# Gate columns of an mLSTM layer moved from a weight slab of their own into the first value slab

## The chip, the core and the metric

The kernel runs on one core of one Trainium2 chip. The metric is the device time of one execution in microseconds (us), as a median of runs. Three runs of the kernel before took 798.25, 798.49 and 798.56 us. Engines are named as the profile names them: PE multiplies matrices (PEld is its loading of the stationary operand), DVE is VectorE, ACT is ScalarE, POOL is GpSimd, and SP issues the weight loads.

## What is computed

Two transformer-like blocks run one after the other over 256 tokens of width 1024, in float32. The first has differential attention, retention, an MLP and a per-layer embedding. The second has an mLSTM, an up projection with a causal convolution, and a down projection. The change lies in the mLSTM's input projection. Cut to what matters, the reference is:

```python
proj = x @ w_in                      # [256, 1024] @ [1024, 3080]
q = proj[..., :512] * dqk ** -0.5    # 4 heads of 128
k = proj[..., 512:1024]
v = proj[..., 1024:2048]             # 4 heads of 256
o_gate = sigmoid(proj[..., 2048:3072])
log_i = proj[..., 3072:3076] + b_gates[:4]                # 8 gate columns
log_f = log_sigmoid(proj[..., 3076:] + b_gates[4:])
# from log_i and log_f: running sums and maxima over the tokens, which give
# the decay that weights the scores q k^T of each head before they meet v
```

The input `x` of this projection is normalized. The norm's factor, one number per token, is not put on `x` but on the products: queries, keys, values and gates are each multiplied by it when they are taken out of PSUM.

## The kernel before

**Weights.** All weights stream through the chip once, in slabs. A slab is 1024 rows by 256 columns and comes in two halves of 512 KB, each with 4 row blocks of 128 rows. `_plan` lists the slabs in the order of use, and `order` lists the halves. A half goes through three rings of buffers: `raw` (5 buffers, filled by SP's load, L151), `hi` (6 buffers: ACT writes the part that a float32r product keeps, L163) and `lo` (6 buffers: DVE writes the rest, L175). A load may start when the `lo` of the half five places earlier is done, and a `hi` or `lo` when PE has used the half six places earlier. Each product is done in three matmuls: high times high, low activations times high weights, and high activations times low weights.

**Order of the work.** Nothing is reordered at run time: each engine works through its instructions as they were written out. `step_b` keeps a block of weights stationary and streams 256 tokens (the result has features on partitions: queries, keys, gates); `step_a` keeps the activations stationary and streams 256 weight columns (the result has tokens on partitions: values). After each half `slot` writes out the next high and low parts and advances what the other engines have pending. `joint` runs two slabs whose last row blocks come late. It leaves its closing work, the statistic of the norm and the taking out of its two products, to a `tail` that is written out after the first half of the next slab.

**Around the change.** `joint(["mq0", "mk0"], ...)` makes the first queries and keys. The next slab, `mg`, holds the 8 gate columns alone, padded to 64 columns, in two loads of 128 KB. In its middle the tail multiplies the sums of squares with a matrix of ones (`pv_n4`, L981 and L982). From `pv_n4` DVE and ACT make the factor of the norm: `m4`, `v5`, a logarithm and an exponential on ACT, one Newton step, `rr` and `rrq` (L989 to L997). Only then can DVE take the first queries and keys out of PSUM (`post_scaled`, L538: `mqk<-ps_mq`, `mqk<-ps_mk`). After `mg` come `mq1`, `mk1` and four value slabs `mv0` to `mv3`. The gates go through `post_mg`, `gates2` (running sums), `gates3` (small transposes to tokens on partitions, `acol`) and, behind `mv1`, `decay_pe` and `decay_post` (the weights `dm` of the scores). The scores of heads 0 and 1 also come behind `mv1`, and meet the values (`my0`, `my1`) behind `mv3`.

**PSUM.** It has 8 banks; the kernel gives 4 to `mmbank` (the products of slabs) and 4 to `aux` (everything small). Within each kind the banks go round: the fifth request gets the bank of the first, and its first matmul has to wait until that bank has been read. Here `ps_mg` is an `aux` bank, so the products that follow the slab pairs take `mmbank`s in the order `pg2`, `pg3`, `mq0`, `mk0`, `mq1`, `mk1`, `mv0`, ...

Of the kernel before, what the change touches and what calls it, by code (L numbers as in the profile page):

```python
# [37 lines left out]
def _plan():  # L38
    slabs = []
    index = {}  # L40

    def slab(name, w, k0, nk, cl):
        index[name] = len(slabs)
        slabs.append((name, w, k0, nk, cl))

    for j in (0,):
        slab("q0", "w_in", 0, 8, 0)
        slab("k0", "w_in", 0, 8, 1024)
    for j in range(4):
# [12 lines left out]
    for j in range(16):  # L62
        slab(f"f1_{j}", "w_ff1", 0, 8, 256 * j)
    for j in range(4):
        for kg in range(4):
            slab(f"f2_{j}_{kg}", "w_ff2", 8 * kg, 8, 256 * j)
    slab("wp", "w_ple", 0, 2, 0)
    for j in range(4):
        slab(f"pg{j}", "w_ple_gate", 0, 8, 256 * j)
    for n in ("mq0", "mk0", "mg", "mq1", "mk1"):  # L70
        if n == "mg":
            slab("mg", "l0_mlstm_w_in_2", 0, 8, 3072)
        else:
            slab(n, "l0_mlstm_w_in_2", 0, 8, (512 if n[1] == "k" else 0) + 256 * int(n[2]))
# [24 lines left out]

@with_exitstack  # L100
def block_kernel(ctx: ExitStack, tc: tile.TileContext, I, out):
# [114 lines left out]
    def pe_b(ps, i, xh, xl, ks, m, start, stop):  # L216
        """A block of weights stays, the activations pass: out is [features, tokens]."""
# [12 lines left out]
    def pe_a(ps, i, xh, xl, ks, t, start, stop):  # L230
        """The activations stay, the weights pass: out is [tokens, features]."""
# [22 lines left out]
    def after(i, *posts):  # L254
        """The small products due behind slab i; what follows it on the other engines."""
# [8 lines left out]
    def halves(i, piece):  # L264
        for s in range(2):
# [77 lines left out]
    with tc.manual_schedule():  # L343
        S.preload_act_table_set(LNEXP)
# [640 lines left out]
        def r4_post():  # L985
            # with 1 / r4^2 = m4 + eps, both norms are (m5 + eps (m4 + eps))^-0.5
# [21 lines left out]
        def post_mg(ps):  # L1008
            gi = wk("gi", 384, tag="aT")[0:4, 0:T]
            gf = wk("gf", 384, tag="aT")[0:4, 0:T]  # L1010
            V.tensor_tensor(out=gi, in0=ps[0:4, 0:T], in1=rr[0:4, :], op=ALU.mult)
            V.tensor_tensor(out=gf, in0=ps[32:36, 0:T], in1=rr[32:36, :], op=ALU.mult)
            V.tensor_scalar(out=gi, in0=gi, scalar1=par[0:4, goff["gates"]:goff["gates"] + 1], scalar2=None, op0=ALU.add)
            V.tensor_scalar(out=gf, in0=gf, scalar1=par[0:4, goff["gates"] + 1:goff["gates"] + 2], scalar2=None, op0=ALU.add)
# [121 lines left out]
        def xnorm():  # L1136
            # x becomes the first block's output
# [22 lines left out]
        for j in range(4):  # L1160
# [54 lines left out]
        def h7_split(j):  # L1215
            """The normalized input; the first slabs take the input as it is and their products the factor."""
# [209 lines left out]
def _columns(a):  # L1426
    """A vector with its entries down the partitions: [128, n / 128]."""
# [3 lines left out]
def _packed(inputs):  # L1431
# [3 lines left out]
    gates[0:4] = f["l0_mlstm_b_gates_2"].reshape(2, 4).T  # L1435
# [5 lines left out]
    for h, (i, s) in enumerate(order):  # L1441
        name, key, k0, nk, cl = slabs[i]
        kk, cw = nk // 2, 2048 // nk
        m = f[key][0] if f[key].ndim == 3 else f[key]
        rows = m[(k0 + s * kk) * P:(k0 + (s + 1) * kk) * P]
        if name == "mg":
            v = w[h, :, 0:256].reshape(P, kk, 64)
            g = rows[:, cl:cl + 8].reshape(kk, P, 8).transpose(1, 0, 2)
            v[:, :, 0:4], v[:, :, 32:36] = g[:, :, 0:4], g[:, :, 4:8]
        else:  # L1450
            w[h] = rows[:, cl:cl + cw].reshape(kk, P, cw).transpose(1, 0, 2).reshape(P, kk * cw)
# [26 lines left out]
```

## Time and profile before

| what | value |
|---|---|
| runs | 798.25, 798.49, 798.56 us; median 798.49 |
| span of the profiled execution, first to last instruction | 796.7 us, mean granted clock 0.998 |
| runs' median less this span | 1.8 us |
| PE busy | 787.4 us, 99% |
| DVE busy | 570.3 us, 72% |
| ACT busy | 464.2 us, 58% |
| weights loaded | 140.25 MB on SP's queue |
| `mg` on PE | from 507.74 us, `mq1` follows at 511.42 us |

The profiled execution's own total is not given apart from its span; the 1.8 us between the span and the median of the runs lie around the instructions. A time such as 507.74 is counted from the first instruction of the span. In a row of the timeline the first number is the start, the second the duration, both in us; the duration of a matmul includes its way through the array, so what one costs is the distance to the start of the next. "x2" joins neighbours of the same kind, and what stands in brackets is idle time ahead of the row and what ended it.

### The profile page before, as it was taken

To read this page: it belongs to the slowest core of one execution; us is meant where nothing else is said; L and a number is where in the kernel's file an instruction comes from. 1 tells how busy PE (TensorE), PEld (TensorE's weight loads), DVE (VectorE), ACT (ScalarE), POOL (GpSimd) and SP (SyncE) were. 2 spreads that over 40 slices of the span, in tenths; PEclk is the share of its full clock that TensorE was granted. 3 is DMA by queue.
4 is the path that set the end of the run, shared out by engine and by line. 5 is a ranking of instruction groups with operands and counts; after the bars stand their busy time and mean duration, and the time that the engine had idled before them with its cause. 6 is when DMAs were issued, how large, how long until landed. Compare 5 with 4: busy or idle time off the path is not lost.

```text
span 796.7 us, 15746 instructions
## 1 busy us (share of the span) xinstructions
PE 787.4 (99%) x6416; PEld 773.2 (97%) x6416; DVE 570.3 (72%) x898; ACT 464.2 (58%) x785; POOL 1.9 (0%) x7
## 2 busy tenths in 40 slices
PE   8999999999999999999999999999999999999996
PEld 8999999999999999999999999999999999999885
DVE  6976889566666577666555557897978988987443
ACT  7655656765744456555444456755865766756432
POOL 0000000000000000000000000000000000000000
PEclk9999999999999999999999999999999999999999
DMA  8775454555666556665666645465374457765621
GB/s 297 274 238 164 151 158 129 149 161 162 188 196 187 172 181 195 190 188 188 199 185 188 181 145 166 136 205 169 121 220 160 143 178 235 221 203 166 206 80 53
DMA packets 40615, 141.97 MB, mean 178 GB/s; under 512 B 4656, under 2 KB 5296, under 8 KB 40544
## 3 DMA queue, kind: packets, MB, share of 16 engines
q1 hardware_dynamic: 40176, 140.25, 55.7%
q8 instruction: 50, 0.82, 0.4%
q0 software_dynamic: 224, 0.72, 0.2%
q14 instruction: 21, 0.17, 0.1%
q10 hardware_dynamic: 144, 0.00, 0.0%
HBM read 139.91 MB, written 1.05 MB: 177 GB/s over the span
## 4 chain that ended last, share of the span: by engine, by line
PE 97%; ACT 1%; DMA 1%; issue 0%; DVE 0%; SPq 0%
PE ps_f L227 8%; PE ps_f L226 8%; PE ps_f L228 8%; PE ps_uv L226 3%; PE ps_ug L226 3%; PE ps_ug L227 3%; PE ps_uv L227 3%; PE acc L1313 3%; PE acc L1315 3%; PE acc L1314 3%; PE ps_ug L228 3%; PE ps_uv L228 3%; PE ps_vr L238 1%; PE ps_va L238 1%; PE ps_mo L238 1%; PE ps_wo L227 1%
## 5 line engine op out<-in xcount | busy, mean ns | idle before, releaser
L175 DVE TENSOR_TENSOR lo_f<-raw_f,hi_f 128x1024 fp32r<-128x1024 f32 x64 | 77.7, 1222 | 52.9 <-ACT hi_f L163 52.9
L163 ACT ACTIVATE hi_f<-raw_f 128x1024 fp32r<-128x1024 f32 x64 | 67.6, 1060 | 79.6 <-PE ps_f L227 70.3
L227 PE MATMUL ps_f<-al,hi_f 128*128 128x256 f32 x256 | 72.1, 282 | 0.0
L226 PE MATMUL ps_f<-ah,hi_f 128*128 128x256 f32 x256 | 72.0, 281 | 0.0
L228 PE MATMUL ps_f<-ah,lo_f 128*128 128x256 f32 x256 | 72.0, 281 | 0.0
L226 PE MATMUL ps_f<-h2h,hi_f 128*128 128x256 f32 x256 | 71.9, 281 | 0.0
L227 PE MATMUL ps_f<-h2l,hi_f 128*128 128x256 f32 x256 | 71.9, 281 | 0.0
L228 PE MATMUL ps_f<-h2h,lo_f 128*128 128x256 f32 x256 | 71.8, 281 | 0.0
L226 PEld LDWEIGHTS ps_f<-ah,hi_f 128*128 128x128 f32 x256 | 48.3, 189 | 0.0
L228 PEld LDWEIGHTS ps_f<-ah,lo_f 128*128 128x128 f32 x256 | 48.3, 189 | 0.0
L226 PEld LDWEIGHTS ps_f<-h2h,hi_f 128*128 128x128 f32 x256 | 48.3, 189 | 0.0
L227 PEld LDWEIGHTS ps_f<-al,hi_f 128*128 128x128 f32 x256 | 48.2, 188 | 0.0
L227 PEld LDWEIGHTS ps_f<-h2l,hi_f 128*128 128x128 f32 x256 | 48.1, 188 | 0.0
L228 PEld LDWEIGHTS ps_f<-h2h,lo_f 128*128 128x128 f32 x256 | 48.1, 188 | 0.0
L175 DVE TENSOR_TENSOR lo_dn<-raw_dn,hi_dn 128x1024 fp32r<-128x1024 f32 x22 | 26.9, 1223 | 22.8 <-ACT hi_dn L163 22.8
L163 ACT ACTIVATE hi_dn<-raw_dn 128x1024 fp32r<-128x1024 f32 x22 | 23.3, 1061 | 30.7 <-PE acc L1314 24.5
L226 PE MATMUL ps_ug<-h7h,hi_ug 128*128 128x256 f32 x144 | 40.8, 283 | 0.0
L226 PE MATMUL ps_uv<-h7h,hi_uv 128*128 128x256 f32 x144 | 40.5, 282 | 0.0
L227 PE MATMUL ps_uv<-h7l,hi_uv 128*128 128x256 f32 x144 | 40.3, 280 | 0.0
L227 PE MATMUL ps_ug<-h7l,hi_ug 128*128 128x256 f32 x144 | 40.3, 280 | 0.0
L228 PE MATMUL ps_ug<-h7h,lo_ug 128*128 128x256 f32 x144 | 40.0, 278 | 0.0
L228 PE MATMUL ps_uv<-h7h,lo_uv 128*128 128x256 f32 x144 | 40.0, 278 | 0.0
(490 smaller groups left out, 2940.9 us busy)
## 6 DMA issues: line engine op xcount, KB each, us to landing
raw_f<-in_w_dram SPq DMA_DIRECT2D x64, 512.0 KB, 3.6
raw_ug<-in_w_dram SPq DMA_DIRECT2D x22, 512.0 KB, 4.2
raw_uv<-in_w_dram SPq DMA_DIRECT2D x22, 512.0 KB, 4.3
raw_dn<-in_w_dram SPq DMA_DIRECT2D x22, 512.0 KB, 3.8
raw_va<-in_w_dram SPq DMA_DIRECT2D x8, 512.0 KB, 5.2
raw_vr<-in_w_dram SPq DMA_DIRECT2D x8, 512.0 KB, 3.5
raw_gr<-in_w_dram SPq DMA_DIRECT2D x8, 512.0 KB, 3.5
raw_ga<-in_w_dram SPq DMA_DIRECT2D x8, 512.0 KB, 3.6
```

The source lines that it names most:

```text
L163: S.activation(hi_t[i, s], raw_t[i, s], ACTF.Copy)
L175: V.tensor_tensor(out=lo_t[i, s], in0=raw, in1=hi_t[i, s].bitcast(F32), op=ALU.subtract)
L226: TE.matmul(o, lhsT=hv[:, a, sl], rhs=xh[:, x, :], start=st, stop=False, skip_group_check=True)
L227: TE.matmul(o, lhsT=hv[:, a, sl], rhs=xl[:, x, :], start=False, stop=False, skip_group_check=True)
L228: TE.matmul(o, lhsT=lv[:, a, sl], rhs=xh[:, x, :], start=False, stop=sp, skip_group_check=True)
L238: TE.matmul(o, lhsT=xh[:, k, ts], rhs=hv[:, a, :], start=st, stop=False, skip_group_check=True)
L1313: TE.matmul(o, lhsT=gh[b][:, r, ts], rhs=hv[:, 0, ns], start=k == 0, stop=False)
L1314: TE.matmul(o, lhsT=gl[b][:, r, ts], rhs=hv[:, 0, ns], start=False, stop=False)
L1315: TE.matmul(o, lhsT=gh[b][:, r, ts], rhs=lv[:, 0, ns], start=False, stop=k == NK - 1)
```

## The change

The slab `mg` is gone. The 8 gate columns stand behind the 256 columns of the first value slab `mv0`, which is now 264 columns wide and comes third, straight behind `mq0` and `mk0`. A raw buffer holds 1024 columns, so this slab is loaded in three pieces, of 3, 3 and 2 row blocks (792, 792 and 528 columns), where the others have two. `step_wide` runs it as `step_a` does, with a bank of PSUM for each half of the tokens, both from `mmbank`. The gates now come out with tokens on partitions: four small ACT copies scale them into `gtok`, and two transposes on PE in the middle of `mk1` turn them. The rest of the gates' work moves back by one place, and the decay and the first scores stand behind `mv2` where they stood behind `mv1`; they still meet the values behind `mv3`.

```diff
-    for n in ("mq0", "mk0", "mg", "mq1", "mk1"):
-        if n == "mg":
-            slab("mg", "l0_mlstm_w_in_2", 0, 8, 3072)
...
-    for j in range(4):
-        slab(f"mv{j}", "l0_mlstm_w_in_2", 0, 8, 1024 + 256 * j)
+    for n in ("mq0", "mk0", "mv0", "mq1", "mk1", "mv1", "mv2", "mv3"):
+        slab(n, "l0_mlstm_w_in_2", 0, 8, {"q": 0, "k": 512, "v": 1024}[n[1]] + 256 * int(n[2]))
...
+def _rows(slab):
+    name, w, k0, nk, cl = slab
+    return ((0, 1, 2), (3, 4, 5), (6, 7)) if name == "mv0" else (tuple(range(nk // 2)), tuple(range(nk // 2, nk)))
+
+def _width(slab):
+    return 264 if slab[0] == "mv0" else 2048 // slab[3]
...
+    def step_wide(name, xh, xl):
+        i = index[name]
+        kk, cw = geometry(i)
+        pss = [mmbank(f"ps_{name}_{t}") for t in range(2)]
+        def piece(s):
+            for t in range(2):
+                ts = slice(t * P, (t + 1) * P)
+                for a, k in enumerate(_rows(slabs[i])[s]):
+                    hv, lv = hi_t[i, s], lo_t[i, s]
+                    o = pss[t][:, 0:cw]
+                    TE.matmul(o, lhsT=xh[:, k, ts], rhs=hv[:, a, :], start=k == 0, stop=False, skip_group_check=True)
+                    TE.matmul(o, lhsT=xl[:, k, ts], rhs=hv[:, a, :], start=False, stop=False, skip_group_check=True)
+                    TE.matmul(o, lhsT=xh[:, k, ts], rhs=lv[:, a, :], start=False, stop=k == 7, skip_group_check=True)
+        halves(i, piece)
+        after(i)
+        return pss
...
-        def post_mg(ps):
+        gtok = wk("gtok", 128, bufs=1)
+        nc.gpsimd.memset(gtok, 0.0)
+        gtokv = gtok.rearrange("p (t n) -> p t n", t=2)
+        def gates0(pss):
+            for t in range(2):
+                for q in range(2):
+                    S.activation(gtokv[:, t, 32 * q:32 * q + 4], pss[t][:, T + 4 * q:T + 4 * q + 4], ACTF.Copy, scale=rrc[:, t:t + 1])
+        def gates1_pe():
+            pg = aux("pg_t")
+            for t in range(2):
+                TE.transpose(pg[0:64, t * P:(t + 1) * P], gtokv[:, t, :], ident)
+            gt["pg"] = pg
...
-        at("mk1", col_pe("c5", rr))
-        at("mk1", col_post("c5", rrc))
-        at("mq1", None, gates2)
-        at("mv0", gates3_pe, gates3_post)
+        def mv0_tail(pss):
+            col_pe("c5", rr)()
+            i = index["mq1"]
+            later(i, col_post("c5", rrc))
+            later(i, lambda: gates0(pss))
+            later(i, lambda: post_halves(mvh, mvl, rrc, [pss[t][:, 0:T] for t in range(2)]))
...
+        at("mk1", gates1_pe, gates1_post, mid=True)
+        at("mk1", None, gates2)
+        at("mv1", gates3_pe, gates3_post)
...
-        for j, n in enumerate(("mv1", "mv1")):
+        for j, n in enumerate(("mv2", "mv2")):
...
-        mlstm(0, "mv1", "mv3")
+        mlstm(0, "mv2", "mv3")
...
-        mlstm(1, "mv1", "mv3")
+        mlstm(1, "mv2", "mv3")
...
-        step_b("mg", h4h, h4l, post_mg)
+        pss0 = step_wide("mv0", h4h, h4l)
+        tails.append((index["mq1"], lambda: mv0_tail(pss0)))
         step_b("mq1", h4h, h4l, post_scaled(mqt, 1, rrq))
```

The instructions of PE between the joint slabs and `mq1`, with the engines that each waits for in brackets; of equal neighbours only the first is shown. `hi_mg_0` is the high part of the gate slab's first half, `ps_mq1` the bank of the second queries. Before:

```order
L228 MATMUL ps_mk0_6160<-h4h_5832,lo_mk0_1_6074 128x256
L226 MATMUL ps_mg_6299<-h4h_5832,hi_mg_0_6102 64x256
L981 MATMUL pv_n4_6312<-sqs_n4_6197,ones_95 128x256 [waits DVE_49]
L982 MATMUL pv_n4_6312<-sqs_n5_6203,ones_95 128x256 [waits DVE_49]
L226 MATMUL ps_mg_6299<-h4h_5832,hi_mg_1_6185 64x256 [waits Activation_49]
L226 MATMUL ps_mq1_6355<-h4h_5832,hi_mq1_0_6233 128x256 [waits Activation_49]
```

Now:

```order
L232 MATMUL ps_mk0_6162<-h4h_5832,lo_mk0_1_6074 128x256
L317 MATMUL ps_mv0_0_6301<-hi_mv0_0_6102,h4h_5832 128x264 [waits PE_49]
L1004 MATMUL pv_n4_6321<-sqs_n4_6199,ones_95 128x256 [waits DVE_49]
L1005 MATMUL pv_n4_6321<-sqs_n5_6205,ones_95 128x256 [waits DVE_49]
L317 MATMUL ps_mv0_0_6301<-hi_mv0_1_6187,h4h_5832 128x264 [waits Activation_49]
L317 MATMUL ps_mv0_0_6301<-hi_mv0_2_6235,h4h_5832 128x264 [waits Activation_49]
L230 MATMUL ps_mq1_6382<-h4h_5832,hi_mq1_0_6253 128x256 [waits DVE_49,PE_49,Activation_49]
```

24 matmuls of `mg` made way for 48 of `mv0`, and the first matmul of `mq1`, which waited for ACT alone (its high part), now waits for DVE and PE as well: `mv0` took the two `mmbank`s that `mq1` and `mk1` had, so `mq1` gets the bank of `mq0`. In the built program this wait is for DVE's instruction `mqk<-ps_mq0`, which reads that bank.

DVE from the end of the statistic (`sqs_n5`) to that instruction; `m4` is the start of the factor's chain, whose eight instructions up to `rrq` are the same in both and are shown by `m4` and `rrq`. Before:

```order
L412 TENSOR_TENSOR sqs_n5_6203<-sqa_n5_5835 128x256
L175 TENSOR_TENSOR lo_mg_1_6205<-raw_mg_1_5972,hi_mg_1_6185 128x256
L175 TENSOR_TENSOR lo_mq1_0_6235<-raw_mq1_0_6007,hi_mq1_0_6233 128x1024
L175 TENSOR_TENSOR lo_mq1_1_6253<-raw_mq1_1_6039,hi_mq1_1_6251 128x1024
L175 TENSOR_TENSOR lo_mk1_0_6295<-raw_mk1_0_6076,hi_mk1_0_6293 128x1024
L989 COPY m4_6315<-pv_n4_6312 128x256
L997 TENSOR_SCALAR rrq_6130<-rr_6128 128x256
L538 TENSOR_TENSOR mqk_6134<-ps_mq0_6159,rrq_6130 128x512
```

Now:

```order
L435 TENSOR_TENSOR sqs_n5_6205<-sqa_n5_5835 128x256
L179 TENSOR_TENSOR lo_mv0_1_6207<-raw_mv0_1_5972,hi_mv0_1_6187 128x792
L179 TENSOR_TENSOR lo_mv0_2_6237<-raw_mv0_2_6007,hi_mv0_2_6235 128x528
L179 TENSOR_TENSOR lo_mq1_0_6255<-raw_mq1_0_6039,hi_mq1_0_6253 128x1024
L179 TENSOR_TENSOR lo_mq1_1_6297<-raw_mq1_1_6076,hi_mq1_1_6295 128x1024
L1012 COPY m4_6324<-pv_n4_6321 128x256
L1020 TENSOR_SCALAR rrq_6130<-rr_6128 128x256
L561 TENSOR_TENSOR mqk_6136<-ps_mq0_6161,rrq_6130 128x512
```

Ahead of `m4` stood a low part of 256 columns and three of 1024; now there stand one of 792, one of 528 and two of 1024.

DVE some 10 us earlier, between the squares of the first four feature blocks and the low parts of the next two (`h4l`). Before:

```order
L409 TENSOR_TENSOR sqa_n5_5835<-sqa_n5_5835,sq_n5_1_6119 128x512
L175 TENSOR_TENSOR lo_mg_0_6123<-raw_mg_0_5920,hi_mg_0_6102 128x256
L959 TENSOR_TENSOR pgs2_6072<-pgs2_6072,pw_5754 128x512
L961 TENSOR_TENSOR x0_73<-x0_73,pgs2_6072 128x512
L953 TENSOR_TENSOR pgs3_6145<-ps_pg3_6041,r3_5755 128x512
```

Now:

```order
L432 TENSOR_TENSOR sqa_n5_5835<-sqa_n5_5835,sq_n5_1_6119 128x512
L179 TENSOR_TENSOR lo_mv0_0_6123<-raw_mv0_0_5920,hi_mv0_0_6102 128x792
L982 TENSOR_TENSOR pgs2_6072<-pgs2_6072,pw_5754 128x512
L984 TENSOR_TENSOR x0_73<-x0_73,pgs2_6072 128x512
L976 TENSOR_TENSOR pgs3_6147<-ps_pg3_6041,r3_5755 128x512
```

The low part in second place has 792 columns where it had 256. On ACT the high part `hi_mv0_0` likewise has 792 columns where `hi_mg_0` had 256; it stands ahead of these squares.

More of the change, by code (lines that the diff above doesn't have):

```diff
@@ L93, in _plan @@
         if n not in paired:
-            order += [(i, 0), (i, 1)]
+            order += [(i, s) for s in range(len(_rows(slabs[i])))]
         elif any(n == g[0] for g in JOINT):
@@ L140, in geometry @@
     def geometry(i):
-        name, w, k0, nk, cl = slabs[i]
-        return nk // 2, 64 if name == "mg" else 2048 // nk
+        return len(_rows(slabs[i])[0]), _width(slabs[i])
     def dma_to(n):
@@ L146, in dma_to @@
             i, s = order[state["dma"]]
-            name, w, k0, nk, cl = slabs[i]
-            kk, cw = geometry(i)
+            name = slabs[i][0]
+            kk, cw = len(_rows(slabs[i])[s]), _width(slabs[i])
             raw = wpool.tile([P, 1024], F32, tag="raw", name=f"raw_{name}_{s}", bufs=NRAW)
@@ L158, in high_to @@
             i, s = order[state["high"]]
-            kk, cw = geometry(i)
+            kk, cw = len(_rows(slabs[i])[s]), _width(slabs[i])
             dma_to(state["high"] + 1)
@@ L169, in split_to @@
             i, s = order[state["split"]]
-            kk, cw = geometry(i)
+            kk, cw = len(_rows(slabs[i])[s]), _width(slabs[i])
             high_to(state["split"] + 1)
@@ L264, in halves @@
     def halves(i, piece):
-        for s in range(2):
+        for s in range(len(_rows(slabs[i]))):
             need(i, s)
@@ L280, in step_b @@
         i = index[name]
-        ps = (aux if name == "mg" else mmbank)(f"ps_{name}")
-        nm = 1 if name == "mg" else 2
+        ps = mmbank(f"ps_{name}")
         def piece(s):
-            for m in range(nm):
-                pe_b(ps, i, xh, xl, range(4 * s, 4 * s + 4), m, s == 0 and m == 0, s == 1 and m == nm - 1)
+            for m in range(2):
+                pe_b(ps, i, xh, xl, range(4 * s, 4 * s + 4), m, s == 0 and m == 0, s == 1 and m == 1)
         halves(i, piece)
@@ L1006, in block_kernel, with gates1_post @@
         gt = {}
-        def post_mg(ps):
+        gtok = wk("gtok", 128, bufs=1)
[10 more added lines that the diff above has]
+            gt["pg"] = pg
+        def gates1_post():
+            pg = gt.pop("pg")
             gi = wk("gi", 384, tag="aT")[0:4, 0:T]
             gf = wk("gf", 384, tag="aT")[0:4, 0:T]
[L1011 to L1014, printed above, removed]
+            V.tensor_scalar(out=gi, in0=pg[0:4, 0:T], scalar1=par[0:4, goff["gates"]:goff["gates"] + 1], scalar2=None, op0=ALU.add)
+            V.tensor_scalar(out=gf, in0=pg[32:36, 0:T], scalar1=par[32:36, goff["gates"] + 1:goff["gates"] + 2], scalar2=None, op0=ALU.add)
             l = wk("gl", 512, tag="qt")[0:4, 0:T]
@@ L1140, in xnorm, with post_halves @@
                                        op0=ALU.mult, op1=ALU.mult)
-        at("mk1", col_pe("c5", rr))
-        at("mk1", col_post("c5", rrc))
-        at("mq1", None, gates2)
-        at("mv0", gates3_pe, gates3_post)
+        def mv0_tail(pss):
[4 more added lines that the diff above has]
+            later(i, lambda: post_halves(mvh, mvl, rrc, [pss[t][:, 0:T] for t in range(2)]))
+        def post_halves(dh, dl, rc, pts):
+            for t in range(2):
+                S.activation(dh[:, t, 0:T], pts[t], ACTF.Copy, scale=rc[:, t:t + 1])
+            yield
+            for t in range(2):
+                V.scalar_tensor_tensor(out=dl[:, t, 0:T], in0=pts[t], scalar=rc[:, t:t + 1], in1=dh[:, t, 0:T].bitcast(F32),
+                                       op0=ALU.mult, op1=ALU.subtract)
+        at("mk1", gates1_pe, gates1_post, mid=True)
+        at("mk1", None, gates2)
+        at("mv1", gates3_pe, gates3_post)
         at("mo0", None, r4_late)
-        for j, n in enumerate(("mv1", "mv1")):
+        for j, n in enumerate(("mv2", "mv2")):
             at(n, lambda j=j: decay_pe(j), lambda j=j: decay_post(j))
-        mlstm(0, "mv1", "mv3")
+        mlstm(0, "mv2", "mv3")
         mlstm(2, "mv3", "mo0")
         mlstm(3, "mv3", "mo0")
-        mlstm(1, "mv1", "mv3")
+        mlstm(1, "mv2", "mv3")
         at("mo1", None, xnorm)
@@ L1156, in block_kernel @@
         joint(["mq0", "mk0"], h4h, h4l, r4_pe, r4_post, [post_scaled(mqt, 0, rrq), post_scaled(mkt, 0, rr)])
-        step_b("mg", h4h, h4l, post_mg)
+        pss0 = step_wide("mv0", h4h, h4l)
+        tails.append((index["mq1"], lambda: mv0_tail(pss0)))
         step_b("mq1", h4h, h4l, post_scaled(mqt, 1, rrq))
         step_b("mk1", h4h, h4l, post_scaled(mkt, 1, rr))
-        for j in range(4):
+        for j in range(1, 4):
             step_a(f"mv{j}", h4h, h4l, post_tok_split(mvh, mvl, j, rrc, 514 * (j // 2) + 258 * (j % 2)))
@@ L1434, in _packed @@
     gates = np.zeros((P, 2), np.float32)
-    gates[0:4] = f["l0_mlstm_b_gates_2"].reshape(2, 4).T
+    gates[0:4] = gates[32:36] = f["l0_mlstm_b_gates_2"].reshape(2, 4).T
     par = [_columns(f[n]) for n, _ in GAINS]
@@ L1442, in _packed @@
         name, key, k0, nk, cl = slabs[i]
-        kk, cw = nk // 2, 2048 // nk
+        ks, cw = _rows(slabs[i])[s], _width(slabs[i])
+        kk = len(ks)
         m = f[key][0] if f[key].ndim == 3 else f[key]
[L1445 to L1451, printed above, removed]
+        rows = m[(k0 + ks[0]) * P:(k0 + ks[0] + kk) * P]
+        cols = rows[:, cl:cl + cw] if name != "mv0" else np.concatenate([rows[:, cl:cl + T], rows[:, 3072:3080]], axis=1)
+        w[h, :, 0:kk * cw] = cols.reshape(kk, P, cw).transpose(1, 0, 2).reshape(P, kk * cw)
     return {
```

2 lines of the change are left out of this document (removed).

## The prediction

> **What bounds the kernel now.** I read first the page's busy shares and its chain, then PE's waits.
>
> ```profile
> PE 787.4 (99%) x6416; PEld 773.2 (97%) x6416; DVE 570.3 (72%) x898; ACT 464.2 (58%) x785; POOL 1.9 (0%) x7
> ...
> PE 97%; ACT 1%; DMA 1%; issue 0%; DVE 0%; SPq 0%
> ```
> ```profile
> PE ps_q L226 <- ACT hi L443: 1.2, 2, 0.8
> ```
>
> PE is busy for 787.4 of 796.7 us, the chain that ended last is 97% PE, and the longest wait between products is 0.8 us, at the start. So time is PE's instructions plus PE's pauses: a matmul less is a gain, and any wait put in front of PE is a loss in full. The span (796.7) and the median of the runs (798.49) differ by 1.8 us around the instructions; I make the sum on the span and add the same difference.
>
> **What PE saves and gains.** First the stretch of `mg`, on PE's timeline, then two rows that price a matmul of 258 columns and two that price a pair of transposes.
>
> ```profile
> 507.74 0.28 PE L226 MATMUL ps_mg<-h4h,hi_mg 128*64 128x256 f32 x1
> ...
> 509.15 0.59 PE L981 MATMUL pv_n<-sqs_n,ones 128*128 128x256 f32 x2
> 509.58 0.59 PE L982 MATMUL pv_n<-sqs_n,ones 128*128 128x256 f32 x2
> ...
> 511.42 0.28 PE L226 MATMUL ps_mq<-h4h,hi_mq 128*128 128x256 f32 x1
> ```
> ```profile
> 552.91 0.28 PE L238 MATMUL ps_mo<-hi_mo,h4h 128*128 128x256 f32 x1
> ...
> 558.64 0.28 PE L532 MATMUL my<-mvh,ws_m 128*128 128x258 f32 x1
> ...
> 560.79 0.28 PE L238 MATMUL ps_mo<-hi_mo,h4h 128*128 128x256 f32 x1
> ```
> ```profile
> 522.78 0.38 PE L477 MATMUL pc_c<-ident,rr 128*128 128x128 f32 x2
> ...
> 523.11 0.28 PE L239 MATMUL ps_mv<-hi_mv,h4l 128*128 128x256 f32 x1
> ```
>
> From 507.74 to 511.42 are 3.68 us; the two `pv` products take 0.43 each (509.15 to 509.58), so the 24 matmuls of `mg` take 2.82, or 0.118 each. They used 64 of the array's columns at the price of 128. They go: **-2.82**. The 48 matmuls of `mv0` are only moved, but are 264 columns wide. 48 of 256 columns take 0.1194 each (552.91 to 558.64), and 18 of 258 the same 0.1194 (558.64 to 560.79). No row has 264. Below, the bound is nothing; above, pro rata: 8 of 256 columns are 0.0037 us, 48 times **+0.18**, which I take. Two transposes more: from 522.78 to 523.11 stand two transposes and one matmul, 0.33 less 0.12 is **+0.21**. So far PE has 2.43 us less to do. The gate copies on ACT and the memset on POOL lie beside PE's work: the transposes come only after `mk1`'s first half, some 5.7 us (48 matmuls) behind those that give the column of factors.
>
> **A wait that grows.** PE already pauses a little before the last row blocks of `mq0`, for `h4l` from DVE.
>
> ```profile
> 501.94 0.39 PE L227 MATMUL ps_mq<-h4l,hi_mq 128*128 128x256 f32 x1
> ```
> ```profile
> 493.26 0.42 ACT L163 ACTIVATE hi_mg<-raw_mg 128x256 fp32r<-128x256 f32 x1 [1.18 <-PE ps_pg L227]
> 493.58 1.69 ACT L418 ACTIVATE h4h<-x,gfg 128x256 fp32r<-128x256 f32 x4
> ...
> 497.55 0.89 ACT L407 ACTIVATE sq_n<-x,par 128x256 f32<-128x256 f32 x2
> ...
> 504.59 0.40 ACT L163 ACTIVATE hi_mg<-raw_mg 128x256 fp32r<-128x256 f32 x1
> ...
> 515.79 2.94 ACT L163 ACTIVATE hi_mv<-raw_mv 128x1024 fp32r<-128x1024 f32 x3
> ```
> ```profile
> 497.68 1.49 DVE L409 TENSOR_TENSOR sqa_n<-sqa_n,sq_n 128x512 f32<-128x512 f32 x2 [0.97 <-ACT sq_n L404]
> 499.08 0.42 DVE L175 TENSOR_TENSOR lo_mg<-raw_mg,hi_mg 128x256 fp32r<-128x256 f32 x1
> 499.42 0.68 DVE L959 TENSOR_TENSOR pgs<-pgs,pw 128x512 f32<-128x512 f32 x1
> ...
> 501.41 0.88 DVE L420 SCALAR_TENSOR_TENSOR h4l<-x,gfg,h4h 128x256 fp32r<-128x256 f32 x2
> ```
>
> Ahead of `h4l` stands the first piece's preparation, which is 792 columns now. On ACT 256 columns take 0.32 (493.26 to 493.58) and 1024 take 0.95 (two steps of the three in 2.94, the last lasting 1.04 to its end), so 792 take 0.76, **0.44** more. The second of DVE's two sums at 497.68 waits for ACT's squares (497.55 + 0.89 = 498.44, and 499.17 less 0.69 is 498.48): it comes 0.44 later. On DVE 256 columns take 0.34 (499.08 to 499.42) and 1024 take 1.14 (rows below), so 792 take 0.89, **0.55** more. Nothing on DVE is idle from there to `h4l`, so PE, which waits for it already, waits **+0.99** longer. If the ACT part were hidden it would be +0.55.
>
> **A wait that is new.** `mq1` gets the bank of `mq0`, and has to wait until DVE has read it, which needs the factor of the norm. DVE's rows of that chain:
>
> ```profile
> 508.75 0.42 DVE L412 TENSOR_TENSOR sqs_n<-sqa_n 128x256 f32<-128x256 f32 x1
> 509.09 0.41 DVE L175 TENSOR_TENSOR lo_mg<-raw_mg,hi_mg 128x256 fp32r<-128x256 f32 x1
> 509.42 2.35 DVE L175 TENSOR_TENSOR lo_mq<-raw_mq,hi_mq 128x1024 fp32r<-128x1024 f32 x2
> 511.69 1.22 DVE L175 TENSOR_TENSOR lo_mk<-raw_mk,hi_mk 128x1024 fp32r<-128x1024 f32 x1
> 512.83 0.41 DVE L989 COPY m<-pv_n 128x256 f32<-128x256 f32 x1
> ...
> 517.00 0.69 DVE L538 TENSOR_TENSOR mqk<-ps_mq,rrq 128x512 f32<-128x512 f32 x1
> ```
>
> Before, `mq1` started at 511.42 and the bank of `mq0` was read by 517.69, which nobody waited for: with `mg` in an `aux` bank the slab pair had banks to spare. Now, in the span's clock:
> - PE is 0.99 late and starts `mv0` at 508.73. All 48 matmuls at 0.1231 (5.91) and the `pv` pair (0.86) bring it to `mq1` at **515.50**.
> - The statistic is 0.99 late, and 0.44 more, because the second piece's high part, which stands ahead of the last four squares on ACT (`hi_mg` at 504.59 before), also has 792 columns. `sqs_n5` starts at 508.75 + 1.43 = 510.18, ends at 510.60, and `pv` is reached at 508.73 + 18 x 0.1231 = 510.95: no wait there.
> - Behind `sqs_n5` DVE has 0.34, then low parts of 792 (0.89), 528 (0.62), and twice 1024 (2.27): `m4` at 514.30, against 512.83. Both high parts lie ready on ACT, and the `pv` pair is done at 511.8.
> - From `m4` to the end of `mqk<-ps_mq` are 517.69 - 512.83 = 4.86 us, which no edit touches. The bank is free at 519.16, and PE goes on some 0.05 later, as after `h4l` (501.41 + 0.48 of one of the pair, 501.94): **519.21**.
>
> PE pauses for **+3.71**. Queued behind `mq1` on PE are its own transposes of `rr` and so the column of factors; all that follows moves with it. `mk1` gets the bank of `mk0`, which DVE reads next, and comes 48 matmuls later.
>
> **What could be late next.** The scores now have one value slab less between decay and `my0`.
>
> ```profile
> 535.07 0.38 PE L1062 MATMUL mm<-mp,pick 4*128 4x256 f32 x1
> ...
> 537.53 0.36 PE L238 MATMUL ps_mv<-hi_mv,h4h 128*128 128x256 f32 x1
> ```
> ```profile
> 537.35 2.67 DVE L1071 SCALAR_TENSOR_TENSOR dm<-mm,acol,maskT 128x256 f32<-128x256 f32 x8
> ...
> 543.53 0.56 DVE L525 TENSOR_TENSOR ws_m<-w_m,ws_m 128x384 fp32r<-128x384 f32 x1 [0.59 <-ACT ws_m L524]
> ```
>
> From the decay's start PE has 2.46 us of decay and scores and 5.73 of `mv3`, 8.2 in all. DVE needs 543.53 + 0.56 - 537.35 = 6.74 from its first `dm`, which came 2.28 behind PE's decay. At that lag `my0` would wait 0.8; but in that lag DVE was doing low parts, which the pause lets it finish early. With 0.7 of lag there is no wait. I take 0, and keep 0.8 as the upper bound.
>
> **Sum.** -2.82 + 0.18 + 0.21 + 0.99 + 3.71 = +2.27 on the span: 799.0, and with the 1.8 around it **800.8 us**, 0.28% slower. With the lower bounds (no widening -0.18, and 0.55 for 0.99, which shifts both sides of the new wait alike) it is +1.65; with `my0` late +3.1. So the forecast's own range is 800.1 to 801.6.
>
> **Rivals.** *The clock falls in the pause (18%).* The rows at the end of the span, behind PE's last matmul (789.75 + 0.28), and at its start:
>
> ```profile
> 792.00:793.00 1.00, 0.00 (x0) 0.00 (x0) 0.87 (x4) 0.52 (x1) 0.00 (x0) 1.00 0.00 0
> 793.00:794.00 1.00, 0.00 (x0) 0.00 (x0) 0.00 (x0) 0.21 (x1) 0.00 (x0) 0.89 0.15 57
> 794.00:795.00 1.00, 0.00 (x0) 0.00 (x0) 0.00 (x0) 0.00 (x0) 0.00 (x0) 0.50 1.02 383
> ```
> ```profile
> 789.75 0.28 PE L1315 MATMUL acc<-lo_dn,gh 128*128 128x256 f32 x1
> ```
> ```profile
> 1.05 4.21 PE L365 MATMUL warm<-ones 128*128 128x128 f32 x18 [1.05 <-DVE epst L362]
> 5.63 0.38 PE L226 MATMUL ps_q<-hh,hi 128*128 128x256 f32 x1 [0.37 <-ACT hi L443]
> ...
> 7.11 0.28 PE L226 MATMUL ps_q<-hh,hi 128*128 128x256 f32 x1
> ```
>
> The granted clock is whole until 793, 0.89 in the next slice and 0.50 after: it fell near 793.8, 3.75 us behind the last matmul. My pause is 3.71, so it is at the edge. At the start six matmuls took 7.11 - 5.63 = 1.48 us, 0.25 each in place of 0.118, 6 us after the first. If the pause sets PE back to that, the loss lies between these six (0.77) and half of 1.05 to 7.11 (3.0): 801.6 to 803.8, middle 802.7. Against it: the pause has to outlast the edge, and every other pause here is too short to tell.
>
> [...]
>
> *The bank is free in time (7%).* If `mq1` found a bank that was read, or the factor came 3.7 us earlier, the sum would be -2.82 + 0.18 + 0.21 + 0.99 = -1.44: 797.05; with the 0.55, 796.6. For it speaks that DVE is busy for only 72% of the span and ACT for 58%. Against it: DVE works in order, and two low parts of `mq1` (2.27) stand ahead of `m4` whatever PE does. It decides from a pause under 1.4.
>
> *A shorter pause (10%).* If the chain overlaps `mv0` better, by up to 2 us, it ends at 798.8 to 800.1.
>
> **How the numbers follow.** Forecast 65%, clock 18%, shorter pause 10%, free bank 7%. 0.2% of 798.49 is 1.6 us, about what a measurement tells from no change. Slower than 800.1: forecast, clock, 0.83 in all; within: 0.13 from the shorter pause and half of the free bank; faster: 0.04. Range: 799.6 to 803.6.
>
> **What would show it.** A pause of PE of 3.3 to 4.1 us at the first `mq1` matmul, released by DVE's `mqk<-ps_mq`, shows the new wait; a gap ahead of the matmul on `h4l` (501.94 before) grown by 1.0 shows the other; `mq1` matmuls at 0.25 in place of 0.118, or a granted clock under 1, show the clock; 48 `mv0` matmuls in over 6.0 us show a dearer width. The prediction is wrong if `mq1` follows `mv0` without a pause, or if `my0` waits.

## The result, and the profile after

The changed kernel takes **802.41 us** (median of four runs, 802.10 to 802.92) against 798.37 for the kernel before (798.16 to 798.56): a ratio of 1.0051, with an interval of 1.0038 to 1.0063. It is slower by 4.0 us. The forecast was 800.8 us, slower by 2.3. The profiled execution took 802.1 us, its span 800.3; around the span lie the same 1.8 us as before.

PE has less to do and loses time all the same. From the page and from PE's waits:

```profile
PE 786.9 (98%) x6394; PEld 772.5 (97%) x6394; DVE 569.9 (71%) x895; ACT 464.7 (58%) x788; POOL 2.2 (0%) x8
...
PE 95%; ACT 2%; DMA 1%; DVE 1%; issue 0%; SPq 0%; DVEq 0%; ACTq 0%
```
```profile
PE ps_mq L230 <- ACT hi_mv L167: 3.8, 1, 3.8
...
PE ps_mq L230 <- ACT h4h L441: 0.6, 1, 0.6
```

The two lower lines are new. Where the time went can be fenced in by two products that both kernels have, the first of `mq0` and the first of `mo0`. The groups of PE's products by line, the kernel before first (the last two times are the first and the last start of the group):

```profile
L226 PE MATMUL ps_mq<-h4h,hi_mq x32: 277/280/285, 496.0 to 516.7; 128*128 128x256 f32 x32
L238 PE MATMUL ps_mo<-hi_mo,h4h x64: 279/284/367, 552.9 to 578.5; 128*128 128x256 f32 x64
```
```profile
L230 PE MATMUL ps_mq<-h4h,hi_mq x32: 277/280/552, 495.7 to 526.1; 128*128 128x256 f32 x32
L242 PE MATMUL ps_mo<-hi_mo,h4h x64: 279/284/367, 556.6 to 582.2; 128*128 128x256 f32 x64
```

Before, 56.9 us lie between them; after, 60.9. So the whole loss of 4.0 us arises here. PE's timeline of the changed kernel inside this stretch:

```profile
502.68 0.38 PE L231 MATMUL ps_mq<-h4l,hi_mq 128*128 128x256 f32 x1
...
508.46 0.29 PE L317 MATMUL ps_mv<-hi_mv,h4h 128*128 128x264 f32 x1
...
510.64 0.59 PE L1004 MATMUL pv_n<-sqs_n,ones 128*128 128x256 f32 x2
...
515.02 0.28 PE L319 MATMUL ps_mv<-lo_mv,h4h 128*128 128x264 f32 x1
519.06 0.55 PE L230 MATMUL ps_mq<-h4h,hi_mq 128*128 128x256 f32 x1 [3.76 <-ACT hi_mv L167]
519.41 0.41 PE L231 MATMUL ps_mq<-h4l,hi_mq 128*128 128x256 f32 x1
...
521.97 0.37 PE L231 MATMUL ps_mq<-h4l,hi_mq 128*128 128x256 f32 x1
522.17 0.28 PE L232 MATMUL ps_mq<-h4h,lo_mq 128*128 128x256 f32 x1
...
523.36 0.38 PE L500 MATMUL pc_c<-ident,rr 128*128 128x128 f32 x2
```

`mv0` ends at 515.02, and `mq1` begins at 519.06: the pause that was forecast. What the forecast's likeliest case did not have stands right behind it. From 519.41 to 521.97 are 12 steps of 0.213 us each, where the same product took 0.118 before and takes it again from 522.17. The granted clock says why. Windows of the trace, cut at the clock's two changes and one step of 3.41 us further at a time (after the length of a window stand PE's busy time, then those of PEld, DVE, ACT and POOL; the clock is the third number from the end):

```profile
511.91:515.32 3.41, 3.39 (x28) 3.18 (x27) 3.28 (x5) 0.03 (x1) 0.00 (x0) 1.00 0.82 291
515.32:518.74 3.42, 0.00 (x0) 0.00 (x0) 2.38 (x6) 3.39 (x5) 0.00 (x0) 1.00 0.89 323
518.74:522.15 3.41, 3.09 (x14) 3.12 (x15) 3.04 (x4) 1.20 (x2) 0.00 (x0) 0.50 0.20 24
522.15:525.56 3.41, 3.41 (x31) 3.41 (x30) 1.78 (x3) 1.25 (x6) 0.00 (x0) 1.00 0.82 280
```

The clock falls to a half 0.32 us before PE goes on, and is whole again after 3.41 us. DVE's rows show what PE waited for:

```profile
502.14 0.89 DVE L443 SCALAR_TENSOR_TENSOR h4l<-x,gfg,h4h 128x256 fp32r<-128x256 f32 x2
...
511.78 2.35 DVE L179 TENSOR_TENSOR lo_mq<-raw_mq,hi_mq 128x1024 fp32r<-128x1024 f32 x2
514.05 0.42 DVE L1012 COPY m<-pv_n 128x256 f32<-128x256 f32 x1
...
518.22 0.69 DVE L561 TENSOR_TENSOR mqk<-ps_mq,rrq 128x512 f32<-128x512 f32 x1
```
```profile
501.60 0.91 ACT L441 ACTIVATE h4h<-x,gfg 128x256 fp32r<-128x256 f32 x2 [2.08 <-DVE x L984]
...
517.95 1.99 ACT L167 ACTIVATE hi_mv<-raw_mv 128x1024 fp32r<-128x1024 f32 x2
```

`mqk<-ps_mq` ends at 518.91 and PE goes on at 519.06. The profile names ACT's `hi_mv` as the releaser, because the first of that pair happens to end near 518.95; it is a high part of `mv1`, which `mq1` doesn't use. That DVE's reading of the bank is meant had to be shown by the runs below. The other new line, 0.6 us on ACT's `h4h`, is part of the older wait: the product ahead of the one on `h4l` now waits too, and ACT's `h4h` waits in its turn for DVE's `x`, which stands behind the first low part of `mv0`.

### The profile page after: what moved, and what is told of

Read it like the earlier page. It is cut to its first block, busy times and chain, and to the rows that moved or that the text cites. A ratio compares the mean times of both kernels' runs of the same rounds, so it can differ in the third digit from the quotient of the medians.

```text
span 800.3 us, 15703 instructions
## 1 busy us (share of the span) xinstructions
PE 786.9 (98%) x6394; PEld 772.5 (97%) x6394; DVE 569.9 (71%) x895; ACT 464.7 (58%) x788; POOL 2.2 (0%) x8
## 4 chain that ended last, share of the span: by engine, by line
PE 95%; ACT 2%; DMA 1%; DVE 1%; issue 0%; SPq 0%; DVEq 0%; ACTq 0%
PE ps_f L231 8%; PE ps_f L230 8%; PE ps_f L232 8%; PE ps_uv L230 3%; PE ps_ug L230 3%; PE ps_ug L231 3%; PE ps_uv L231 3%; PE acc L1368 3%; PE acc L1366 3%; PE acc L1367 3%; PE ps_ug L232 3%; PE ps_uv L232 3%; PE ps_vr L242 1%; PE ps_va L242 1%; PE ps_mo L242 1%; PE ps_wo L231 1%
```

## The experiments

All times are medians; each ratio is to the kernel before, run on the same occasion.

| run | edit | us | ratio, interval |
|---|---|---|---|
| e1 | 28 products in the pause | 800.79 | 1.0030 (1.0019 to 1.0042) |
| e2 | `mv0`'s banks from `aux` | 798.21 | 0.9997 (0.9988 to 1.0006) |
| e3 | factor's chain earlier on DVE | 798.78 | 1.0004 (0.9996 to 1.0013) |
| e4 | e2 and e3 | 796.91 | 0.9982 (0.9973 to 0.9991) |
| e5 | e4, first piece of 264 columns | 798.51 | 1.0002 (0.9993 to 1.0011) |
| e6 | 6 products in the pause | 802.38 | 1.0052 (1.0039 to 1.0065) |
| e7 | 3 products in the pause | 802.47 | 1.0053 (1.0040 to 1.0065) |
| e8 | kernel before, `mg` and a product in `mmbank`s | 799.23 | 1.0011 (1.0002 to 1.0020) |
| e9 | the changed kernel again | 803.21 | 1.0059 (1.0046 to 1.0072) |
| e10 | 12 products in the pause | 802.47 | 1.0044 (1.0031 to 1.0056) |
| e11 | e8, the product's bank held | 806.77 | 1.0105 (1.0091 to 1.0118) |
| e12 | e4, pieces 2-3-3, squares first | 796.34 | 0.9975 (0.9965 to 0.9985) |

### The pause and the clock apart: e1

```diff
         halves(i, piece)
         after(i)
+        fill = aux("fill")
+        for _ in range(28):
+            TE.matmul(fill[:, 0:T], lhsT=xh[:, 0, 0:P], rhs=xh[:, 0, :], start=True, stop=True)
         return pss
```

> The changed kernel with 28 more products of 256 columns between mv0 and mq1, into a spare bank that nobody reads; it computes the same, does only more. Theory (the pause ends by the bank of mq0, and PE's clock falls inside it): mq1 starts when it did, since its bank comes free as before, but PE is idle for 3.76 - 28 x 0.118 = 0.46 us only, so the first 24 matmuls of mq1 take 2.85 us and not 4.30. Time 802.41 - 1.45 = 800.96. Rival (the slow matmuls of mq1 have another cause at that place, such as DVE and ACT at the banks or the weights): they stay slow, 802.4.

Measured: 800.79 us. PE's idle time at that place is down to 0.4, and the clock is whole where it was at a half (PE's waits, and one window):

```profile
PE ps_mq L230 <- ACT hi_mv L167: 0.4, 1, 0.4
```
```profile
519.00:520.00 1.00, 0.99 (x8) 1.00 (x9) 1.00 (x2) 0.90 (x1) 0.00 (x0) 1.00 0.00 0
```

`mq1` starts no earlier (519.01 in its trace), yet the kernel is 1.6 us faster, by doing more. So the lower clock is a cost of its own, and without it the change takes what the forecast said: 800.8.

### What makes the pause: e2, e3, e4

e2 takes `mv0`'s two banks from the other ring. e3 leaves the banks and writes the start of the factor's chain, `m4` to `v`, ahead of `mq1`'s two low parts on DVE; the first of these then fills DVE's wait for ACT inside the chain, and the second comes behind `mqk`. From `mq0`'s start to the end of the Newton step a cap holds the ordinary splitting back at `mq1`'s first half, and `need` puts single halves where they are wanted. e4 does both. Of the diffs, the first is that of e2 and the second that of e3; the second's last line is in e4 alone.

```diff
-        pss = [mmbank(f"ps_{name}_{t}") for t in range(2)]
+        pss = [aux(f"ps_{name}_{t}") for t in range(2)]
```
```diff
-        split_to(state["done"] + NBUF)
+        split_to(min(state["done"] + NBUF, state["cap"]))
...
             S.activation(y0, y0, ACTF.Exp, scale=-0.5)
+            need(index["mq1"], 0)
             newton(v, y0, T, "n5", rr, eps=0.0)
+            state["cap"] = 10 ** 6
+            need(index["mk1"], 1)
```

> The changed kernel with mv0's two banks taken from the ring aux, as mg's was; nothing else. Theory (the pause is the wait for the bank of mq0): mq1 follows mv0 at once, no pause of 3.76 and no lower clock. But DVE's chain is not faster: rr is ready at 517.85, PE comes to its transposes at 516.45 and waits about 1.45 there, and mk1's first low part (ready at 520.6 in the changed kernel) may cost up to 1.1 more. 802.41 - 3.76 - 1.45 + 1.45 = 798.65, up to 799.75. Rival (the factor chain holds PE whatever the bank, as everything behind needs it): 801 to 802.4.

> The changed kernel with its banks, but DVE's order around the factor changed: the three operations from m4 to v come ahead of mq1's two low parts, of which one goes between v and the Newton steps and one behind mqk. Theory (the pause is as long as DVE's chain makes it, and the clock falls only behind a pause over some 3.7): mqk<-ps_mq ends at 516.7 rather than 518.9, the pause is 1.85, the clock stays whole: 802.41 - 1.9 - 1.45 = 799.05, up to 799.3 if the second low part comes late. Rival (a lower clock follows any pause of a microsecond or two): 800.5. Rival (the two low parts are not what delays the chain): 802.4.

> Both: mv0's banks from aux, and the factor's chain ahead of the low parts (here mq1's second and mk1's two stand ahead of mqk). Theory: no pause at mq1 and none at the transposes of rr; of the change's terms remain -2.82 + 0.12 + 0.21 + 0.99 against 798.37, so 796.9, and up to 0.8 more where DVE's low parts of mq1 and mv1 come late: 796.9 to 797.7, faster than both kernels. Rival (DVE is the bound of this stretch once PE does not pause, so that its low parts make PE wait as long elsewhere): 798.5 to 800.

Measured: 798.21, 798.78 and 796.91 us. PE's waits that are left in the stretch, in e2, e3 and e4:

```profile
PE pa_g L1082 <- ACT me L1072: 1.1, 1, 1.1
...
PE ps_mq L230 <- ACT h4h L441: 0.6, 1, 0.6
```
```profile
PE ps_mq L230 <- DVE mqk L563: 1.6, 1, 1.6
...
PE ps_mq L230 <- ACT h4h L443: 0.6, 1, 0.6
```
```profile
PE ps_mq L230 <- ACT h4h L443: 0.6, 1, 0.6
```

With other banks the pause at `mq1` is gone (e2). With the same banks and an earlier chain it is 1.6, and here, with no high part ending beside it, the profile names `mqk` itself (e3). Both together leave nothing of it (e4). The wait is for the bank, and its length is the chain's; the two low parts ahead of `m4` were 2.2 us of it (3.76 less 1.60). Behind e3's pause the granted clock is 1.00 (517.66 to 521.07 in its trace).

e2's wait was expected at the transposes of `rr`, by an error of mine: half a slab is 24 products, not 12, so PE comes to them 2.8 us behind `mq1`'s start, when `rr` is ready. It came 16 us later instead, at the gates' transposes, whose input comes late from ACT and DVE. In the changed kernel PE comes there some 5 us later, after the pause and the low clock, and finds it ready (538.19 against 534.20). e4's time is the sum of the terms that remain: 798.41 - 2.82 + 0.08 + 0.22 + 1.0 = 796.9.

### The bank alone: e8 and e11

In the kernel before, `mg` keeps its order and width, but takes a bank of the slabs' ring, and one product more takes another. In e11 that product's bank is also read late, by the last two lines.

```diff
-        ps = (aux if name == "mg" else mmbank)(f"ps_{name}")
+        ps = mmbank(f"ps_{name}")
+        if name == "mg":
+            two = state["two"] = mmbank("ps_mg_2")
+            TE.matmul(two[:, 0:T], lhsT=xh[:, 0, 0:P], rhs=xh[:, 0, :], start=True, stop=True)
...
         def post_mg(ps):
+            jk2 = wk("jk2", 4, bufs=1)
+            V.tensor_copy(jk2, state.pop("two")[:, 0:4])
```

> The kernel before with only the banks changed: mg's products go to a bank of the ring of the slabs instead of aux, and one product more (that nobody reads) takes another, so that mq1 gets the bank of mq0 as in the changed kernel; order, widths and DVE's work stay. Theory (the bank alone makes the pause, and a pause over some 3.7 lets the clock fall): mq1 waits from 511.54 to the end of mqk<-ps_mq at 517.69 and 0.15 more: 6.2 of idle time; with 0.12 for the product and 1.45 for the clock 798.4 + 0.1 + 6.2 + 1.45 = 806.2. If the loss by the clock grows with the pause, more: up to 808. Rival (it takes mv0 and its gates to make PE wait): 798.5.

> As e8, but the additional product's bank is read by DVE behind the norm's factor (four columns, beside mg's own bank), so that both stay taken until then, as mv0's do. In e8 the bank of the additional product was free at once and went to mq1, and only mk1 waited. Theory (the bank alone makes the pause): mq1 waits from 511.5 to the end of mqk<-ps_mq at 517.7, idle for 6.0 to 6.2 us, and the clock falls for one window or two: 798.4 + 0.1 + 6.2 + 1.5 to 3.2 = 806.2 to 807.9. Rival (the order or widths of mv0 are needed too): 799.2 as e8.

Measured: 799.23 and 806.77 us. PE's new waits, in e8 and in e11:

```profile
PE ps_mk L226 <- ACT hi_mv L163: 0.5, 1, 0.5
```
```profile
PE ps_mq L226 <- ACT hi_mv L163: 6.1, 1, 6.1
```

e8 missed: only `mk1` waited, for 0.5. In its trace `mk1` goes on at 517.45, behind the end of `mqk<-ps_mq` at 517.31, so `mk1` got the bank of `mq0`, and `mq1` that of the additional product, which nobody reads. With that bank held until DVE is past the factor (e11), `mq1` waits for 6.1 us with the old order, the old widths and no value slab near. It goes on at 517.64, again 0.15 us behind the end of `mqk<-ps_mq` at 517.49. So the bank is enough by itself.

### The wait for h4l: e5 and e12

e5 shortens the first piece to one row block (and puts the statistic's products behind the second piece). e12 takes pieces of 2, 3 and 3 and holds the second piece's parts back behind the last squares: the cap stands at that piece and bounds the high parts too. Both start from e4; the lower part of the diff is e12's alone.

```diff
-    return ((0, 1, 2), (3, 4, 5), (6, 7)) if name == "mv0" else ...
+    return ((0,), (1, 2, 3), (4, 5), (6, 7)) if name == "mv0" else ...    # e5
+    return ((0, 1), (2, 3, 4), (5, 6, 7)) if name == "mv0" else ...       # e12
...
-        high_to(state["done"] + NBUF)
+        high_to(min(state["done"] + NBUF, state["cap"]))
...
             pv = store.pop("pv4")
+            need(index["mv0"], 2)
+            high_to(order.index((index["mq1"], 0)) + 1)
             m4 = wk("m4", T, tag="ysq")
```

> The kernel of e4 with mv0 in four pieces of 1, 3, 2 and 2 row blocks (264, 792, 528, 528 columns) in place of three, and the statistic's products behind the second piece. Theory (the wait for h4l grew by 0.99 because the first piece's preparation on ACT and DVE grew from 256 to 792 columns): with 264 columns there the wait ahead of mq0's last row blocks goes back to what it was before the change; 796.91 - 0.99 = 795.9, and up to 0.3 more if the statistic's products wait. Rival (that wait comes from elsewhere, such as the table load or the residual's chain on DVE): 796.9.

> e4 with mv0 in pieces of 2, 3 and 3 row blocks (528, 792, 792 columns), and the second piece's high and low parts behind the last squares of the statistic instead of ahead of them. Theory: the first piece costs ACT 0.22 and DVE 0.30 less ahead of h4l, so PE waits 0.5 less there; the squares come 0.75 earlier, which keeps the statistic's products and the second piece's low part in time for a first piece of 12 matmuls in place of 18. 796.91 - 0.5 = 796.4. Rival (as in e5 the wait comes back behind the shorter first piece, at the statistic's products or at the second low part): 796.9 or more.

Measured: 798.51 and 796.34 us. In e5 the wait named `h4h` is gone from the list, as expected, and the matmul on `h4l` stands 5.95 us behind `mq0`'s start (501.87 and 495.92), as it did before the change; but two other waits stand there:

```profile
PE ps_mv L319 <- DVE lo_mv L179: 1.7, 1, 1.7
...
PE pa_g L1087 <- ACT me L1077: 0.6, 1, 0.6
```

A first piece of 6 products is over before DVE has finished the sums and the second piece's low part. So the term of 1.0 is real, but cannot be taken back by shortening the piece alone: -1.0 + 1.7 + 0.6 gives 1.3 of the 1.6 us by which e5 is slower than e4; the rest stays open. e12 keeps both sides in step. Its matmul on `h4l` stands 6.4 us behind `mq0`'s start, not 6.9 (the group of `mq0`'s products, and PE's timeline):

```profile
L230 PE MATMUL ps_mq<-h4h,hi_mq x32: 277/280/384, 495.8 to 520.2; 128*128 128x256 f32 x32
```
```profile
502.20 0.38 PE L231 MATMUL ps_mq<-h4l,hi_mq 128*128 128x256 f32 x1
```

It gains 0.57 us on e4 (0.48 when each is set against its own runs of the kernel before) and 2.0 on the kernel before, and no wait in the stretch is left in its list: -2.82 + 0.08 + 0.22 + 0.5 = -2.0. The change's idea is worth that much, with other banks and DVE's order.

### When the clock falls: e6, e7, e9, e10

e6, e7 and e10 are e1 with 6, 3 and 12 products in place of 28; e9 is the changed kernel on another occasion.

> The changed kernel with 6 products of 256 columns into a spare bank between mv0 and mq1: PE is idle for 3.76 - 6 x 0.118 = 3.05 us instead of 3.76, the time at which the bank comes free is the same. Theory (the clock falls a fixed 3.4 to 3.8 us behind the last product, 3.44 in the changed kernel's trace and 3.75 at the end of the span before): no fall, 800.8 as with 28 products. Rival (the clock falls by its own windows or already behind a shorter pause): mq1's first products slow in the trace, and 801.5 to 802.4 in at least some of the executions.

> The same with 3 products: PE is idle for 3.41 us. If the clock falls 3.44 us behind the last product, this is just too short: 800.8. If it falls earlier in some executions, the times lie between 800.8 and 802.4, and spread.

> The changed kernel itself again, on another occasion. In the traces so far the granted clock changes at ends of windows of 3.413 us that run on through the span, and their place in the span differs from trace to trace. Theory (a window has to be idle for the most part only, as in e6, where 3.05 of the 3.41 us were idle): the pause of 3.76 fills most of one window wherever it lies, or large parts of two, so all executions lie between 802.0 and 803, and none at 800.8. Rival (a window has to be idle as a whole, and the first four executions were luck): most executions at 800.8, since 3.76 holds a whole window of 3.41 in one of ten positions.

> The changed kernel with 12 products of 256 columns into a spare bank between mv0 and mq1: PE is idle for 3.76 - 12 x 0.118 = 2.35 us, which is 69% of a window at most. e3's pause of 1.6 us (47% of one window) left the clock whole. Theory (a window counts as idle from somewhere between 47% and 89%): 800.8 if no window counts, 802.4 if one does, and both among the executions if it depends on where the window lies; the trace tells the share at which it did or didn't.

Measured: 802.38, 802.47, 803.21 and 802.47 us. e6 and e7 missed: a pause of 3.05 us already costs as much as one of 3.76, in each of the ten executions. In e9's five executions the times are 802.08 and 803.18 to 803.51. In e10's five they are 800.84, 800.99 and three of 802.47 to 802.55: with 2.3 us idle, the clock fell in some executions and not in others, if the times are read so; the profiled execution is one of the two shorter ones. In the changed kernel's trace the clock falls at 518.74 and, behind the last product, at 798.63: 82 steps of 3.413 us, as long as the low stretch itself. In e6, e7, e9 and e11, too, the fall in the pause and the one behind the last product lie whole numbers of such steps apart: 81 (519.50 and 795.98), 82 (519.55 and 799.45), 82 (517.95 and 797.84) and 84 (514.10 and 800.82), each time worked out from the mean clock of slices of 0.25 us. So in these traces the clock changes at such steps, which run on through the span, and a window here is the stretch from one to the next. Their place in the span differs from trace to trace: the changed kernel's clock falls at 518.74 in the first trace and at 517.95 in e9's. Windows of e6, e9 and e10, cut at these steps (e10's clock does not change here, so its cuts are counted back from its only fall, at 797.42):

```profile
516.09:519.50 3.41, 0.36 (x4) 0.23 (x2) 2.90 (x7) 3.41 (x5) 0.00 (x0) 1.00 0.73 293
519.50:522.91 3.41, 3.41 (x18) 3.41 (x18) 2.52 (x3) 0.68 (x1) 0.00 (x0) 0.50 0.25 50
522.91:526.33 3.42, 3.42 (x31) 3.42 (x31) 2.18 (x3) 1.65 (x7) 0.00 (x0) 1.00 0.68 263
```
```profile
514.53:517.95 3.42, 0.55 (x5) 0.33 (x3) 2.32 (x7) 2.86 (x5) 0.00 (x0) 1.00 0.92 352
517.95:521.36 3.41, 2.54 (x12) 2.57 (x13) 3.38 (x5) 1.76 (x2) 0.00 (x0) 0.50 0.12 44
521.36:524.77 3.41, 3.41 (x18) 3.41 (x18) 0.21 (x2) 0.00 (x0) 0.00 (x0) 0.50 0.89 282
524.77:528.19 3.42, 3.42 (x31) 3.42 (x31) 3.42 (x6) 2.91 (x8) 0.00 (x0) 1.00 0.28 89
```
```profile
514.11:517.53 3.42, 2.91 (x25) 2.70 (x23) 2.35 (x7) 1.93 (x4) 0.00 (x0) 1.00 0.95 373
517.53:520.94 3.41, 1.60 (x13) 1.63 (x14) 3.31 (x7) 2.70 (x3) 0.00 (x0) 1.00 0.36 142
520.94:524.35 3.41, 3.41 (x32) 3.41 (x31) 2.81 (x4) 1.15 (x6) 0.00 (x0) 1.00 0.71 197
```

In e6 the clock falls at 519.50, which is 0.2 us after PE has gone on at 519.30: it comes behind a window in which PE was busy for 0.36 of 3.41 us (89% idle). In e9 it falls behind one with 0.55 of 3.42 busy (84% idle), and the next window, 2.54 busy (26% idle), did not lift the clock, so that it stayed low for two windows. In e10's profiled execution the pause lies across two windows, and 1.60 busy (53% idle) left the clock whole in the next. The 0.51 and 1.81 us idle in the two are its 2.3.

## Why the prediction was right, and where it was short

The measured 802.41 us lies inside the stated range of 799.6 to 803.6 us, but outside the forecast's own range of 800.1 to 801.6. The stated range held it because it left room for the rivals: the forecast's sum came true, and the first rival came true on top of it. e1, with the pause nearly filled, shows the forecast's sum alone: 800.79 us.

- **PE's work: right.** `mg`'s 24 products are gone. The 18 products of `mv0` from 508.46 to 510.64 took 0.1211 us each, against 0.1194 for 256 columns: 48 of them cost +0.08, not the +0.18 of the pro rata rule; the lower bound was nearer. But the forecast was wrong to let the lower end of its range gain 0.18 from that bound: `mq1` starts when the bank is free, so a cheaper `mv0` only makes the pause longer.
- **The wait for `h4l`: right, +1.0 for +0.99.** The matmul stands 502.68 - 495.74 = 6.94 us behind `mq0`'s start, against 501.94 - 496.01 = 5.93 before. e5 and e12 show that the first piece's width sets it.
- **The new wait: right, 3.92 for 3.71.** `mq1` would have followed at 515.14 (515.02 and one product) and came at 519.06. Of the difference, 0.1 is PE's going on 0.15 us behind DVE's reading rather than 0.05, and the rest is mostly the cheaper `mv0`, behind which PE is ready sooner. e2, e3, e4 and e11 show bank and chain as its causes.
- **`my0`: right.** It doesn't wait. DVE's first `dm` came 0.77 us behind PE's decay (545.14 and 544.37), near the 0.7 that the forecast asked for, where it was 2.28 before.
- **The clock: this step failed.** The likeliest case had the pause without the clock, and the rival "the clock falls in the pause" got 18%, because "the pause has to outlast the edge" of 3.75 us that one row at the end of the span had shown. The runs show no fixed delay behind the last product: in the changed kernel's trace the clock falls 3.44 us behind it (518.74, the product ending at 515.30), in e11 2.6 us (514.10 and 511.51). In e6 it fell behind a window with a tenth of busy time (0.36 of 3.41 us), behind a pause of 3.05. All nine executions of the changed kernel lie between 802.1 and 803.5, within the rival's 801.6 to 803.8. Its price here: 24 products from 519.06 to 523.36 took 4.30 us in place of 2.83 (24 times 0.118), +1.47; and 2.4 where two windows were low (803.2 less e1's 800.8).

With these, -2.82 + 0.08 + 0.22 + 1.0 + 3.92 + 1.47 = +3.9, where the trace's stretch gives 4.0. The two transposes are the 0.22: from 529.25 to 529.59, less one product.

That a window has to be idle as a whole, the rival in e9, does not hold in these traces: the clock fell behind windows in which PE was busy for 0.36 us (e6), 0.55 (e9) and 0.83 (e11).

## What to carry to other kernels

Where work is moved between two products that share a ring of PSUM banks, count who gets whose bank, and when that bank is read; the price of a shared bank is here the chain of the engine that reads it (a pause of 3.76 us in the changed kernel, of 6.1 in e11, of 1.6 in e3 with the chain earlier). Price a pause of the tensor engine as its length plus the clock: here a pause of 3.05 us or more cost some 1.3 to 2.7 us besides, by execution (the changed kernel's 802.08 to 803.51 less e1's 800.79), one of 2.3 us did so in some executions, by their times, and one of 1.6 us (e3) did not. Filling such a pause with products that nobody needs was a gain (e1, 802.41 to 800.79 us), and writing the late chain ahead of work that can wait was a larger one (e3, to 798.78).

## What the runs showed of the hardware that was not expected

- **The clock stayed whole behind a window that was 53% idle and fell behind one that was 76% idle.** e10 shows the first (1.60 of 3.41 us busy) and e11's pause the second, one trace each; what lies between stays open, and that the share of busy time is what decides, and not something that goes with it, is not shown. e11's windows, from the one in which PE was busy for 0.83 of 3.42 us:

```profile
510.68:514.10 3.42, 0.83 (x8) 0.57 (x5) 3.09 (x5) 0.23 (x1) 0.00 (x0) 1.00 0.97 291
514.10:517.51 3.41, 0.00 (x0) 0.00 (x0) 2.57 (x7) 3.38 (x5) 0.00 (x0) 0.50 0.76 304
517.51:520.92 3.41, 3.28 (x15) 3.31 (x16) 3.38 (x6) 0.07 (x1) 0.00 (x0) 0.50 0.20 24
520.92:524.34 3.42, 3.42 (x31) 3.42 (x30) 3.16 (x5) 2.17 (x4) 0.00 (x0) 1.00 0.91 297
```

- **A low clock was not lifted behind a window that was 26% idle** (e9, 2.54 of 3.41 us busy), and was lifted behind one that was 9% idle (the changed kernel, 3.09 busy). One trace each; where the border lies stays open.
- **At half the clock a product of 256 columns took 0.213 us, not twice 0.118** (12 steps from 519.41 to 521.97 in the changed kernel's trace). So by these two numbers a low window costs 45% of its busy time and not half.
- **Not of the hardware, but of how the program hands out PSUM banks:** the bank that is free first seems to be given out first (e8: `mq1` got the bank that nobody reads), rather than the oldest of the ring, which the description of the kernel before took for granted.
